# Small matmuls that rotate through strips of the array: attention blocks and a block inverse

## The chip, the core and the metric

The kernel runs on one core of a Trainium2 chip. The metric is the device time of one execution in microseconds, the median of several runs. The core has a matmul engine (PE, with PEld for its loads of the stationary operand), a vector engine (DVE), an activation engine (ACT), a general engine (POOL) and a queue that issues transfers (SP). They run side by side and wait for one another by semaphores.

## What is computed

One layer over 2048 latent tokens and 256 context tokens, width 1024: a modulated layer norm, one wide input projection, two linear-attention branches, each in both directions over the tokens, and gated output projections with a residual layer norm. The two places that matter here, cut from the reference:

```python
def gla_chunk_scan(q, k, v, g, s0):          # branch B, f_t and k_t = 1 - f_t
    ...
    qg = q * jnp.exp(G)
    kg = k * jnp.exp(-G)
    attn = jnp.where(incl, jnp.einsum('bhncd,bhnsd->bhncs', qg, kg), 0.0)
    ...
    o_c = einsum(qg_c, S) + einsum(attn_c, v_c)
    S = S * gl_c + einsum(kd_c, v_c)

def gdn_chunk_scan(q, k, v, g, beta, s0):    # branch A, the gated delta rule
    ...
    a_mat = jnp.where(strict, jnp.einsum('bhncd,bhnsd->bhncs', kb, k) * decay, 0.0)
    sol = lax.linalg.triangular_solve(a_mat + eye, rhs, left_side=True, lower=True, unit_diagonal=True)
    ...
```

Branch B needs, per head, direction and chunk, a triangular matrix `attn`. Branch A needs, per head, direction and chunk, the inverse of a unit triangular matrix.

## The kernel before

Everything is fp32. The large projections are three matmuls of a split operand each (`proj`, lines 211 to 213, moving operand 128x512). The small matmuls of this study are plain fp32, and the trace shows each of these as two passes: two records of a weight load and a matmul.

The array can be used in strips of 32. Which strips a matmul takes follows from its operands: the partitions from which it reads its operands give the row strip, the partitions of PSUM to which it writes give the column strip. A stationary operand 32 wide over 128 partitions takes one column strip of four (the profile writes 128*32); one 64 wide takes two (128*64); a 32x32 block takes one row strip and one column strip (32*32), here called a tile of the array.

**Branch B, `scan_group`** (from line 502). For each of 4 heads and 2 directions it goes over 4 groups of 512 latent tokens and one of the context. A latent group holds four chunks of 128 tokens, and each chunk's 128x128 matrix `attn` is made in `pat` (PSUM, four chunks side by side) from blocks: 16 products of 32x32 on the diagonal for the four chunks; then, per chunk `i`, two 32x32 blocks across (k = 0, 1; operands `a` and `b32`) and one 64x64 block across (operands `a64` and `b64`). The helper `mm` sets which operand is stationary: `b` in direction 0, `a` in direction 1. So a block lands on the partitions, and in the column strips, of its `b` tokens in direction 0 and of its `a` tokens in direction 1. When all are done, line 610 copies `pat` under a mask into `atB` (DVE), which line 619 uses. There are 32 latent groups in all. While they run, PE also carries the projections of the next group, of the next head (`head_units`) and of a gate (`gate_units`).

**Branch A, `levels`** (from line 809). The 128x128 inverse of each of 18 chunks is put together from the inverses of its 32x32 diagonal blocks (made by `solve` on DVE): five stages of small matmuls, each followed by a copy out of PSUM.

- L828: 16 matmuls 32x32, four tiles of the array (`pairs`), four heads each, then the copy to `yt` (DVE, L830)
- L834: 8 matmuls 32x32, two tiles, then a copy to `N64` (DVE, L837)
- L840: 16 matmuls 32x32, four tiles, then copies to `Nb` (ACT, L842)
- L847: 8 matmuls 64x64, two tiles (`hs`), then the copy to `yt2` (DVE, L849)
- L852: 8 matmuls 64x64, two tiles, then copies to `Nb` (ACT, L854)

All write to one PSUM tile `lvt` of 128 partitions by 512 floats. In each stage the loop over tiles is outside and the loop over heads inside, so four matmuls in a row use the same tile of the array. Between the stages stand `prep` of later chunks, `stepA` (the recurrence of branch A, line 931) and gate projections (`gate_block`, L211 to L213).

What sets the order: the program is written in stages as above, and a scheduler with its own estimate of times fixes the order on each engine when the kernel is built. On the chip each engine follows that order.

Of the kernel before, what the change touches and what calls it, by code (L numbers as in the profile page):

```python
# [24 lines left out]
H = 4  # L25
# [14 lines left out]
def block_kernel(ctx, tc, x, c, ctx_in, c_ctx, w_mod, b_mod, w_in, conv_w, a_log, dt_bias,  # L40
# [442 lines left out]
    with tc.tile_pool(name="rb", reuse_waits="tile", bufs=1, side="right") as rb, \  # L483
# [12 lines left out]
        def bl(a):  # L496
            return slice(32 * a, 32 * a + 32)

        def b4(t):
            return t.rearrange("p c (b t) -> p c b t", t=32)  # L500

        def scan_group(h, d, g, ps, S):
# [4 lines left out]
            s = rb.tile([P, GT], F32, tag="s", name="s", bufs=2)[:, :n]  # L507
# [51 lines left out]
            a = X.rearrange("p (c t) -> p c t", t=P)  # L559
# [9 lines left out]
            def fb(f, m):  # L569
                return f.unsqueeze(3).to_broadcast([P, k_, m, 32])  # L570
# [18 lines left out]
            if lat:  # L589
                a64 = rb.tile([P, 4, 64], F32, tag="a64", name="a64")  # L590
                b64 = rb.tile([P, 4, 64], F32, tag="b64", name="b64")
                b32 = rb.tile([P, 4, 64], F32, tag="b32", name="b32")
                ve.tensor_tensor(out=b4(a64), in0=b4(a)[:, :, 2:4], in1=fb(f2, 2), op=ALU.mult)
                po.tensor_tensor(out=b4(b64), in0=b4(b)[:, :, 0:2], in1=fb(f3, 2), op=ALU.mult)
                po.tensor_tensor(out=b4(b32), in0=b4(b)[:, :, 0:4:2], in1=fb(f4, 2), op=ALU.mult)

                def mm(i, am, bm, asl, bsl):
                    if d == 0:
                        te.matmul(out=pat[bsl, i, asl], lhsT=bm, rhs=am, start=True, stop=True)
                    else:  # L600
                        te.matmul(out=pat[asl, i, bsl], lhsT=am, rhs=bm, start=True, stop=True)

                for i in range(4):
                    for k in range(4):
                        mm(i, a[:, i, bl(k)], b[:, i, bl(k)], bl(k), bl(k))
                for i in range(4):
                    for k in range(2):
                        mm(i, a[:, i, bl(2 * k + 1)], b32[:, i, bl(k)], bl(2 * k + 1), bl(2 * k))
                    mm(i, a64[:, i, :], b64[:, i, :], slice(64, 128), slice(0, 64))
                ve.copy_predicated(out=atB[d], mask=mk[d].unsqueeze(1).to_broadcast([P, 4, P]), data=pat)  # L610
                o = rb.tile([P, 4, P], F32, tag="o", name="o")
                if d == 1:
                    sy.dma_start(out=o, in_=oP[h, g])
                pw = pb.tile([P, 4, P], F32, tag="o", name="pw")
                qg = ag if d == 0 else bg
# [54 lines left out]
        for h in range(H):  # L670
            fill = head_units(h + 1) if h + 1 < H else gate_units(NEARLY + GA)
            for d in range(2):
                w = load_w((C_FF, C_FB)[d] + h * P)
                S = None
                for j, g in enumerate(((4, 0, 1, 2, 3), (4, 3, 2, 1, 0))[d]):
                    S = scan_group(h, d, g, proj(w, g), S)
                    for _ in range(FBI[d][j] if h + 1 < H else FB[j] * d):
                        next(fill, None)
            for _ in fill:
                pass  # L680
# [18 lines left out]
    with tc.tile_pool(name="rc", reuse_waits="tile", bufs=2, side="right") as rc, \  # L699
# [109 lines left out]
        def levels(pos):  # L809
            ch = seq[pos]  # L810
            Nb, N64 = Nbs[pos % 2], N64s[pos % 2]
            an = rc.tile([P, H, 96], F32, tag="an2", name="an2", bufs=1)
            sy.dma_start(out=an, in_=anD[ch])
            tx = [rc.tile([P, 2, H, 32], F32, tag=f"n{i}", name=f"n{i}", bufs=1) for i in range(2)]
            for i in range(2):
                sy.dma_start(out=tx[i].rearrange("p d h j -> p (d h) j"), in_=nD[i][pos].rearrange("d h b i j -> (b i) (d h) j"))
            n3 = [tx[1 - d][:, d] for d in range(2)]
            nt = [tx[d][:, d] for d in range(2)]
            for b in range(4):
                for d in range(2):  # L820
                    (ve, po)[d].tensor_copy(out=Nb[bl(b), d, :, bl(b)], in_=n3[d][bl(b)])
                ac.copy(out=N64[bl(b), :, bl(b % 2)], in_=nt[b // 2][bl(b)])
            pairs = [(d, 2 * p + d, 2 * p + 1 - d) for d in range(2) for p in range(2)]
            lvt = pc.tile([P, H, 128], F32, tag="lv", bufs=1, name="lvt")
            py, pn = (lvt[:, :, 32 * i:32 * i + 32] for i in range(2))
            for d, s, t in pairs:
                for h in range(H):
                    te.matmul(out=py[bl(t), h, :], lhsT=an[bl(s), h, 0:32], rhs=nt[d][bl(s), h, :], start=True, stop=True)  # L828
            yt = rc.tile([P, H, 64], F32, tag="yt", name="yt", bufs=1)
            ve.tensor_copy(out=yt[:, :, 0:32], in_=py)  # L830
            for d, s, t in pairs:
                if s // 2 == d:
                    for h in range(H):
                        te.matmul(out=pn[bl(t), h, :], lhsT=n3[d][bl(t), h, :], rhs=yt[bl(t), h, 0:32], start=True, stop=True)  # L834
            for d, s, t in pairs:
                if s // 2 == d:
                    ve.tensor_copy(out=N64[bl(t), :, bl(s % 2)], in_=pn[bl(t)])  # L837
            for d, s, t in pairs:
                for h in range(H):
                    te.matmul(out=pn[bl(s), h, :], lhsT=yt[bl(t), h, 0:32], rhs=n3[d][bl(t), h, :], start=True, stop=True)  # L840
            for d, s, t in pairs:
                ac.copy(out=Nb[bl(s), d, :, bl(t)], in_=pn[bl(s)])  # L842
            hs = [(d, slice(64 * d, 64 * d + 64), slice(64 - 64 * d, 128 - 64 * d)) for d in range(2)]
            pn, py = lvt[:, :, 0:64], lvt[:, :, 64:128]
            for d, s, t in hs:
                for h in range(H):
                    te.matmul(out=py[t, h, :], lhsT=an[s, h, 32:96], rhs=N64[s, h, :], start=True, stop=True)  # L847
            yt = rc.tile([P, H, 64], F32, tag="yt", name="yt2", bufs=1)
            ve.tensor_copy(out=yt, in_=py)  # L849
            for d, s, t in hs:  # L850
                for h in range(H):
                    te.matmul(out=pn[s, h, :], lhsT=yt[t, h, :], rhs=Nb[t, d, h, t], start=True, stop=True)  # L852
            for d, s, t in hs:
                ac.copy(out=Nb[s, d, :, t], in_=pn[s])  # L854
            sy.dma_start(out=atN[ch, :, :, 1], in_=Nb)

        grp = [(c0, min(CG, NC - c0)) for c0 in range(0, NC, CG)]
        for i in range(len(grp) + 2):
            pl = list(range(grp[i][0], sum(grp[i]))) if i < len(grp) else []
            ll = list(range(grp[i - LAG][0], sum(grp[i - LAG]))) if 0 <= i - LAG < len(grp) else []  # L860
            if IL == 0:
                for ch in pl:
                    prep(ch)
                for ch in ll:
                    levels(ch)
            elif IL == 3:
                for ch in ll:
                    levels(ch)
                for ch in pl:
                    prep(ch)  # L870
            else:
                while pl or ll:
                    if pl:
                        prep(pl.pop(0))
                    if ll:
                        levels(ll.pop(0))
                        if IL == 2 and ll:
                            levels(ll.pop(0))
            if 0 <= i - LAG + 1 < len(grp):
                solve(*grp[i - LAG + 1])  # L880
# [20 lines left out]
    if True:  # L901
        SA = []
        for d in range(2):
            t = rd.tile([P, H, P], F32, tag=f"S{d}", name=f"S{d}")
# [291 lines left out]
```

## Time and profile before

| | |
|---|---|
| median of 3 runs | 2302.93 us (2299.16 to 2306.05) |
| the profiled execution | 2301.48 us, its span 2299.7 us |
| PE busy | 2201.6 us (96% of the span) |
| DVE, ACT, POOL busy | 1391.9, 912.9, 734.8 us |
| granted PE clock, mean | 0.985 |
| branch B stage | about 525 to 1063 us of the span |
| `levels` | 1225 to 1690 us of the span |

How to read it: a PE row's time is the union of its matmuls, and each matmul's duration holds the pipeline's depth (about 0.19 us for a 32-wide one), so many of them overlap. What a series of matmuls costs is read from the starts: from its first start to the start of the matmul that follows. In a row of the timeline that holds several records, the first column is the first start, the second the time from there to the last end.

### The profile page before, as it was taken

The page shows a single profiled execution, that of the slowest core. Times are in us where ns is not written, and L with a number is a line of the kernel's source. Part 1 is how long each engine was busy: PE and PEld are TensorE (multiplying, and loading weights), DVE is VectorE, ACT ScalarE, POOL GpSimd, SP SyncE. Part 2 cuts the span into 40 slices and gives each one's busy share as a digit, 9 for nine tenths or more (in the row PEclk, how much of TensorE's full clock was granted, in tenths as well). Part 3 has the DMA queues.
Part 4 walks back from the last instruction along what each step waited for, and adds up shares of the span by engine and source line. Part 5 has one row for each costly group of instructions (what it writes and reads, how often), then busy time and mean ns, then how long its engine had stood idle before and what let it go on. Part 6 is the DMA issues. An engine that isn't in the chain of part 4 may idle for free. (4 is left out here: it accounts for less than half of the span.)

```text
span 2299.7 us, 39916 instructions
## 1 busy us (share of the span) xinstructions
PE 2201.6 (96%) x14998; PEld 1843.8 (80%) x14998; DVE 1391.9 (61%) x3198; ACT 912.9 (40%) x2312; POOL 734.8 (32%) x736
## 2 busy tenths in 40 slices
PE   7899999999999999999999999999989988999998
PEld 2778888888888888888877787888878877888887
DVE  5926666627675776784464858774332337766565
ACT  3522222233343443442434454544444345434441
POOL 3614333312221221214544454421114223432331
PEclk8999999999999999999999999999999999999999
DMA  8312222322322322223656577877788765344432
GB/s 317 107 42 72 68 69 74 90 69 68 95 75 71 106 70 82 81 80 114 182 158 185 176 233 248 256 213 209 229 265 281 246 217 188 120 139 136 126 109 78
DMA packets 298328, 330.24 MB, mean 144 GB/s; under 512 B 77535, under 2 KB 216917, under 8 KB 298135
## 3 DMA queue, kind: packets, MB, share of 16 engines
q1 hardware_dynamic: 296119, 320.35, 45.3%
q0 software_dynamic: 2016, 7.34, 0.9%
q8 instruction: 118, 1.93, 0.4%
q14 instruction: 75, 0.61, 0.1%
HBM read 216.83 MB, written 110.79 MB: 142 GB/s over the span
## 5 line engine op out<-in xcount | busy, mean ns | idle before, releaser
L211 PE MATMUL ps<-uhi,wh 128*128 128x512 f32 (+1 forms) x1824 | 707.3, 388 | 6.4 <-DVE uhi L299 2.7
L212 PE MATMUL ps<-ulo,wh 128*128 128x512 f32 (+1 forms) x1824 | 705.4, 387 | 2.8 <-DVE ulo L301 2.6
L213 PE MATMUL ps<-uhi,wl 128*128 128x512 f32 (+1 forms) x1824 | 705.5, 387 | 0.5 <-POOL wl L203 0.5
L211 PEld LDWEIGHTS ps<-uhi,wh 128*128 128x128 f32 x1824 | 345.2, 189 | 72.0 <-DVE uhi L299 3.8
L212 PEld LDWEIGHTS ps<-ulo,wh 128*128 128x128 f32 x1824 | 345.4, 189 | 66.4 <-DVE ulo L301 3.7
L213 PEld LDWEIGHTS ps<-uhi,wl 128*128 128x128 f32 x1824 | 344.9, 189 | 64.0 <-POOL wl L203 0.9
L203 POOL TENSOR_TENSOR wl<-ws,wh 128x512 fp32r<-128x512 f32 x144 | 192.2, 1335 | 536.3 <-ACT wh L202 515.5
L202 ACT CAST wh<-ws 128x512 fp32r<-128x512 f32 x144 | 89.5, 622 | 286.1 <-DMA ws<-in_w_in_dram 193.6
L399 DVE SCALAR_TENSOR_TENSOR acc<-raw,cols,acc 128x512 f32<-128x512 f32 x192 | 153.9, 855 | 0.9
L1095 PE MATMUL py<-yh,wab 128*128 128x256 f32 x512 | 146.1, 287 | 8.5 <-DVE mg L1098 7.6
L1097 PE MATMUL py<-yh,wab 128*128 128x256 f32 x512 | 144.4, 282 | 0.0
L1096 PE MATMUL py<-yl,wab 128*128 128x256 f32 x512 | 144.3, 282 | 0.0
L578 POOL TENSOR_TENSOR bg<-s,fz 128x512 f32<-128x512 f32 (+1 forms) x36 | 37.8, 1049 | 263.4 <-ACT X L558 97.5
L1114 PE MATMUL pso<-uhi,mh 128*128 128x512 f32 x256 | 102.8, 403 | 7.2 <-ACT mh L1100 3.2
L1095 PEld LDWEIGHTS py<-yh,wab 128*128 128x128 f32 x512 | 97.5, 191 | 10.9 <-DVE mg L1098 9.2
L1116 PE MATMUL pso<-uhi,ml 128*128 128x512 f32 x256 | 101.8, 398 | 0.6 <-DVE ml L1101 0.6
L1115 PE MATMUL pso<-ulo,mh 128*128 128x512 f32 x256 | 101.5, 397 | 0.0
L1096 PEld LDWEIGHTS py<-yl,wab 128*128 128x128 f32 x512 | 97.6, 191 | 0.4
L1097 PEld LDWEIGHTS py<-yh,wab 128*128 128x128 f32 x512 | 97.6, 191 | 0.2
L1078 POOL TENSOR_TENSOR yl<-gt,yh 128x512 fp32r<-128x512 f32 x32 | 44.5, 1393 | 149.1 <-ACT yh L1077 149.1
L402 POOL TENSOR_TENSOR acc<-acc,sg 128x512 f32<-128x512 f32 (+1 forms) x56 | 71.5, 1295 | 46.3 <-ACT sg L401 46.3
L1088 ACT ACTIVATE mg<-mg 128x512 f32<-128x512 f32 x64 | 40.4, 632 | 112.0 <-DMA mg<-gT 112.0
(373 smaller groups left out, 4097.8 us busy)
## 6 DMA issues: line engine op xcount, KB each, us to landing
ws<-in_w_in_dram SPq DMA_DIRECT2D x144, 256.0 KB, 3.2
gT<-gt SPq DMA_DIRECT2D x96, 256.0 KB, 3.2
kv<-knvD SPq DMA_DIRECT2D x36, 512.0 KB, 5.2
kq<-qkvD SPq DMA_DIRECT2D x32, 512.0 KB, 5.6
an<-atN SPq DMA_DIRECT2D x32, 512.0 KB, 6.0
mg<-gT SPq DMA_DIRECT2D x64, 256.0 KB, 3.5
qkvD<-acc SPq DMA_DIRECT2D x48, 256.0 KB, 2.3
l<-qkvD SPq DMA_DIRECT2D x16, 768.0 KB, 5.1
```

What stands on the lines that cost most here:

```text
L202: ac.copy(out=wh[:, j:j + 4, :], in_=ws)
L203: po.tensor_tensor(out=wl[:, j:j + 4, :], in0=ws, in1=wh[:, j:j + 4, :].bitcast(F32), op=ALU.subtract)
L211: te.matmul(out=ps, lhsT=wh[:, k, :], rhs=uhi[gi][:, k, :], start=(k == 0), stop=False)
L212: te.matmul(out=ps, lhsT=wh[:, k, :], rhs=ulo[gi][:, k, :], start=False, stop=False)
L213: te.matmul(out=ps, lhsT=wl[:, k, :], rhs=uhi[gi][:, k, :], start=False, stop=(k == KB - 1))
L399: ve.scalar_tensor_tensor(out=a_, in0=raw[:, o + k:o + k + n], scalar=wk, in1=a_, op0=ALU.mult, op1=ALU.add)
L1095: te.matmul(out=py[:, i, :], lhsT=wh[:, k, ms_], rhs=yh[i][:, k, :], start=(k == 0), stop=False)
L1096: te.matmul(out=py[:, i, :], lhsT=wh[:, k, ms_], rhs=yl[i][:, k, :], start=False, stop=False)
L1097: te.matmul(out=py[:, i, :], lhsT=wl[:, k, ms_], rhs=yh[i][:, k, :], start=False, stop=(k == H - 1))
L1114: te.matmul(out=ps, lhsT=mh[:, k, ts_], rhs=wout[0][k][:, ns], start=(k == 0), stop=False)
L1115: te.matmul(out=ps, lhsT=mh[:, k, ts_], rhs=wout[1][k][:, ns], start=False, stop=False)
L1116: te.matmul(out=ps, lhsT=ml[:, k, ts_], rhs=wout[0][k][:, ns], start=False, stop=(k == KB - 1))
```

## The change

Two edits, both on PE alone.

1. In `scan_group`, the 64x64 block across becomes two matmuls with a stationary operand 32 wide and a moving operand 64 wide, so that all blocks use strips of 32. The order of the four matmuls of a chunk is set by direction: column strips 0, 2, 0, 1 in direction 0 and 3, 1, 3, 2 in direction 1.
2. In `levels`, all five loops have the heads outside and the tiles of the array inside.

```diff
+                def across32(i, k):
+                    mm(i, a[:, i, bl(2 * k + 1)], b32[:, i, bl(k)], bl(2 * k + 1), bl(2 * k))
+
+                def across64(i, k):
+                    if d == 0:
+                        mm(i, a64[:, i, :], b64[:, i, bl(k)], slice(64, 128), bl(k))
+                    else:
+                        mm(i, a64[:, i, bl(k)], b64[:, i, :], bl(2 + k), slice(0, 64))
...
                 for i in range(4):
-                    for k in range(2):
-                        mm(i, a[:, i, bl(2 * k + 1)], b32[:, i, bl(k)], bl(2 * k + 1), bl(2 * k))
-                    mm(i, a64[:, i, :], b64[:, i, :], slice(64, 128), slice(0, 64))
+                    across32(i, d)
+                    across32(i, 1 - d)
+                    across64(i, d)
+                    across64(i, 1 - d)
...
-            for d, s, t in pairs:
-                for h in range(H):
+            for h in range(H):
+                for d, s, t in pairs:
                     te.matmul(out=py[bl(t), h, :], lhsT=an[bl(s), h, 0:32], rhs=nt[d][bl(s), h, :], start=True, stop=True)
...
-            for d, s, t in hs:
-                for h in range(H):
+            for h in range(H):
+                for d, s, t in hs:
                     te.matmul(out=py[t, h, :], lhsT=an[s, h, 32:96], rhs=N64[s, h, :], start=True, stop=True)
```

The loops of L834, L840 and L852 change in the same way as those of L828 and L847 shown here. Eleven lines are added ahead of `levels`, so what is L828, L834, L840, L847, L852 before is L839, L845, L851, L858, L863 after.

The order on PE around a group of branch B before (`pk` is a transpose, `pw` the output; `X` and `s` hold `a` and `b`, `b_...` here is `b32` beside `X`, and `b64` beside `a_...`, which is `a64`):

```order
L583 MATMUL pk<-ident,bg 128x128 x4
L599 MATMUL pat<-X,s 32x32 x16
L599 MATMUL pat<-X,b_4169 32x32 x2
L599 MATMUL pat<-a_4167,b_4168 64x64
L599 MATMUL pat<-X,b_4169 32x32 x2
L599 MATMUL pat<-a_4167,b_4168 64x64
```

And such a group after:

```order
L583 MATMUL pk<-ident,bg 128x128 x4
L599 MATMUL pat<-X,s 32x32 x11
L599 MATMUL pat<-X,b_4484 32x32 x2
L599 MATMUL pat<-a_4482,b_4483 32x64 x2
L599 MATMUL pat<-X,b_4484 32x32 x2
L599 MATMUL pat<-a_4482,b_4483 32x64 x2
```

One block of 64x64 has become two of 32x64; what stands around the group is the same, and how many of the 16 diagonal blocks come ahead of the transposes differs from group to group in both kernels.

The order on PE at the first stage of `levels` for one chunk, before (`n` with its two numbers are the two sets of inverted blocks):

```order
L213 MATMUL ps<-uhi_414,wl 128x512
L828 MATMUL lvt<-n_10815,an_10813 32x32 x8
L828 MATMUL lvt<-n_10816,an_10813 32x32 x8
L725 MATMUL pk<-ident,l 128x128 x4
L732 MATMUL pq<-ident,l 128x128 x4
```

And after:

```order
L213 MATMUL ps<-uhi_309,wl 128x512
L839 MATMUL lvt<-n_10943,an_10941 32x32 x2
L839 MATMUL lvt<-n_10944,an_10941 32x32 x2
L839 MATMUL lvt<-n_10943,an_10941 32x32 x2
L839 MATMUL lvt<-n_10944,an_10941 32x32 x2
L839 MATMUL lvt<-n_10943,an_10941 32x32 x2
L839 MATMUL lvt<-n_10944,an_10941 32x32 x2
L839 MATMUL lvt<-n_10943,an_10941 32x32 x2
L839 MATMUL lvt<-n_10944,an_10941 32x32 x2
L736 MATMUL pk<-ident,l 128x128 x4
```

The 16 matmuls of the stage stand together as before and alternate between the sets. The number of gate projections between the last stages of two successive chunks stays within one or two (the count of L211 ahead of the ninth chunk's last stage is 1586 before and 1584 after). On the other engines, rows move by a few places near these points and no instruction is added or removed.

More of the change, by code (lines that the diff above doesn't have):

```diff
@@ L830, in levels @@
             ve.tensor_copy(out=yt[:, :, 0:32], in_=py)
-            for d, s, t in pairs:
-                if s // 2 == d:
-                    for h in range(H):
+            for h in range(H):
+                for d, s, t in pairs:
+                    if s // 2 == d:
                         te.matmul(out=pn[bl(t), h, :], lhsT=n3[d][bl(t), h, :], rhs=yt[bl(t), h, 0:32], start=True, stop=True)
@@ L837, in levels @@
                     ve.tensor_copy(out=N64[bl(t), :, bl(s % 2)], in_=pn[bl(t)])
-            for d, s, t in pairs:
-                for h in range(H):
+            for h in range(H):
+                for d, s, t in pairs:
                     te.matmul(out=pn[bl(s), h, :], lhsT=yt[bl(t), h, 0:32], rhs=n3[d][bl(t), h, :], start=True, stop=True)
@@ L844, in levels @@
             pn, py = lvt[:, :, 0:64], lvt[:, :, 64:128]
-            for d, s, t in hs:
-                for h in range(H):
+            for h in range(H):
+                for d, s, t in hs:
                     te.matmul(out=py[t, h, :], lhsT=an[s, h, 32:96], rhs=N64[s, h, :], start=True, stop=True)
@@ L849, in levels @@
             ve.tensor_copy(out=yt, in_=py)
-            for d, s, t in hs:
-                for h in range(H):
+            for h in range(H):
+                for d, s, t in hs:
                     te.matmul(out=pn[s, h, :], lhsT=yt[t, h, :], rhs=Nb[t, d, h, t], start=True, stop=True)
```

## The prediction

> **What bounds the kernel now.** I read the page's busy line first, then the busy time by stages, then who PE waits for in the two stages that the change touches, and last the timeline of PE around one group and one chunk.
>
> ```profile
> PE 2201.6 (96%) x14998; PEld 1843.8 (80%) x14998; DVE 1391.9 (61%) x3198; ACT 912.9 (40%) x2312; POOL 734.8 (32%) x736
> ...
> core 0: us, PE busy (x) PEld busy (x) DVE busy (x) ACT busy (x) POOL busy (x), PEclk, DMA share, GB/s
> 525.00:1063.00 538.00, 535.02 (x4337) 447.63 (x4337) 378.93 (x1030) 215.53 (x393) 121.90 (x125) 1.00 0.28 83
> 1225.00:1690.00 465.00, 445.57 (x4016) 373.22 (x4015) 289.14 (x821) 225.90 (x746) 158.12 (x202) 0.98 0.73 220
> ```
>
> In the branch B stage PE is idle for 3 us of 538, in the `levels` stage for 19 of 465. No other engine is near: DVE has 70% and 62%. The order on each engine is fixed, so in these stages the time is the sum of what PE's instructions take, plus those few waits. The waits themselves, from the list of who waited for whom on PE in each stage:
>
> ```profile
> PE pk L583 <- POOL bg L578: 0.9, 1, 0.9
> PE pat L599 <- ACT s L551: 0.9, 1, 0.9
> PE pS L588 <- DMA v<-vB: 0.7, 1, 0.7
> PE pw L618 <- DVE S L624: 0.4, 1, 0.4
> ...
> PE lvt L852 <- DVE yt L849: 9.4, 6, 2.7
> PE pq L732 <- DVE an L769: 1.7, 1, 1.7
> ```
>
> Four waits in the first stage, each under 1 us: a PE that gets faster there turns that into time. In the second, 6 of the 18 chunks already find `yt` late at L852.
>
> **Part 1, the blocks of branch B.** Timeline of PE over one group in direction 0, and the durations of its matmuls (least, median, most in ns) from the view of the tile `pat`:
>
> ```profile
> 537.17 0.46 PE L599 MATMUL pat<-X,s 128*32 128x32 f32 x32
> 537.45 0.26 PE L599 MATMUL pat<-X,b 128*32 128x32 f32 x4
> 537.63 0.33 PE L599 MATMUL pat<-a,b 128*64 128x64 f32 x2
> 537.89 0.26 PE L599 MATMUL pat<-X,b 128*32 128x32 f32 x4
> 538.08 0.33 PE L599 MATMUL pat<-a,b 128*64 128x64 f32 x2
> 538.33 0.26 PE L599 MATMUL pat<-X,b 128*32 128x32 f32 x4
> 538.52 0.33 PE L599 MATMUL pat<-a,b 128*64 128x64 f32 x2
> 538.78 0.26 PE L599 MATMUL pat<-X,b 128*32 128x32 f32 x4
> 538.96 0.33 PE L599 MATMUL pat<-a,b 128*64 128x64 f32 x2
> 539.22 0.38 PE L618 MATMUL pw<-S,ag 128*128 128x128 f32 x1
> ...
> L599 PE MATMUL pat<-X,s x512: 196/196/218, 524.7 to 1000.0; 128*32 128x32 f32 x171
> ```
>
> The 32 passes of the diagonal, which go round four strips, take 0.46 us to the last end, so 0.46 - 0.196 = 0.26 us from first to last start: 8 passes in each strip, about 32 ns each, four strips side by side. The 24 passes of the blocks across take from 537.45 to 539.22, 1.77 us, in four equal rounds of 0.44 us (537.89, 538.33, 538.78). In a round the four 32-wide passes need 0.26 - 0.20 = 0.06 us between starts; the rest, 0.38 us, goes into two 64-wide passes and the change of shape before and behind them.
>
> After, all 64 passes of a group use strips of 32. Per round there are eight passes, and one strip has four of them (0 in direction 0, 3 in direction 1): two with a moving operand of 32 and two of 64. The first kind takes 32 ns in a strip, as above. The second is not in the trace. Its bounds: as the first (32 ns) or the whole 64-wide pass with its drain, half of 0.38 us. A moving operand of 64 against 32 costs 26 ns by the durations of two 128-row matmuls:
>
> ```profile
> L599 PE MATMUL pat<-a,b x128: 222/246/271, 526.3 to 1003.1; 128*64 128x64 f32 x128
> ```
>
> 222 less 196 is 26, so I take 32 + 26 = 58 ns. A round is then 2 x 32 + 2 x 58 = 180 ns for the busiest strip, with the other strips beside it, four rounds 0.72 us, and some 0.10 us to leave the shape at the end (now 539.22 less the last 64-wide start). 1.77 - 0.82 = 0.95 us per group, 30.4 us over 32 groups; some groups are cut by other matmuls and pay an entry more, in both kernels, so 30 us.
>
> What hides behind this? `atB` is copied by DVE when the last block is done, and an output matmul (L619) waits for it. That copy waits for the blocks and is late for nobody: in the list of the stage no matmul waits for it. With 30 us gone from 538, DVE stands at 379 of 508, 75%, and next to be late would be `bg` (L578) or `s` (L551), the two that PE waited for 0.9 us. I take no loss here, 3 us at most.
>
> **Part 2, the five loops of `levels`.** Four of the stages of one chunk in the timeline, and the durations of their passes from the view of the tile `lvt`:
>
> ```profile
> 1294.45 0.89 PE L828 MATMUL lvt<-n,an 32*32 32x32 f32 x32
> 1299.49 0.59 PE L834 MATMUL lvt<-yt,n 32*32 32x32 f32 x16
> 1305.26 0.89 PE L840 MATMUL lvt<-n,yt 32*32 32x32 f32 x32
> 1310.15 0.96 PE L847 MATMUL lvt<-N,an 64*64 64x64 f32 x16
> ...
> L828 PE MATMUL lvt<-n,an x576: 184/191/258, 1225.0 to 1680.7; 32*32 32x32 f32 x192
> L847 PE MATMUL lvt<-N,an x288: 218/218/308, 1246.0 to 1686.3; 64*64 64x64 f32 x144
> ```
>
> From first to last start: L828 and L840 0.89 - 0.19 = 0.70 us, L834 0.40, L847 0.96 - 0.22 = 0.74. After, L828 and L840 are four tiles with eight passes each, one head of all four tiles at a time: the pattern of the 32 diagonal passes, 0.26 us. Saved: 0.44 each. L834 is two tiles with eight passes each, which is the same series with two strips left out: 0.25, saved 0.15. L847 and L852 are two tiles with eight 64-wide passes each, 8 x 58 = 0.46, saved 0.28 each. Sum 0.44 x 2 + 0.15 + 0.28 x 2 = 1.59 us a chunk, 28.6 us over 18 chunks.
>
> The cover is thinner than in part 1. Behind each stage stands a copy on DVE or ACT that the next stage needs, but gate projections stand between the stages (L828 at 1294.45, L834 at 1299.49: 5 us), so an earlier end seldom changes when the next starts. Where L852 already waits for `yt` (6 of 18 chunks), PE comes earlier and waits longer; the price is between 0 and 6 x 1.59 = 9.5 us, and I take the middle, 5 us. The transfers have 0.73 of their engines in this stage, and would have 0.73 x 465 / 441 = 0.77.
>
> A rule speaks against this part. All tiles of a stage write to one PSUM tile, `lvt`, on different partitions, and their operands lie in different row strips. In the trace two such tiles do run together: L847 has 16 passes of 58 ns, 0.93 us if one followed the other, and takes 0.74; L834 has 16 of 32 ns, 0.51, and takes 0.40; where the loop goes from one tile to the next, their passes overlap. The Trainium skill (TensorEngine Tiling (Array Packing), Gotcha 1: PSUM Pressure) says that different row tiles cannot access the same PSUM bank simultaneously; by that rule the tiles of a stage would take turns and rotating would gain nothing. The trace disagrees for two tiles, and shows nothing of four.
>
> **The sum.** 30 + 28.6 - 5 = 53.6 us off the profiled 2301.48 us is 2248; the median of the runs lies 1.5 us above the profiled one, so 2249, which I round to 2250 us.
>
> **Rivals.**
>
> *Row strips take turns at the one PSUM tile.* Then every pass of `levels` follows the one before it: 32 x 32 = 1.02 us for L828 and L840 (0.32 more than now), 0.51 for L834 (0.11 more), 0.93 for L847 and L852 (0.19 more): 1.13 us x 18 = 20 us lost against the 30 of part 1, 2293. For it: four at once stand nowhere in the trace. Against: the 0.74 and 0.40 above. In a milder form two run together and four do not: L828 and L840 then take 0.51, 0.19 saved each, the rest as forecast, 1.09 x 18 = 20 us, and 2302.9 - 30 - 20 + 5 = 2258, which lies inside the main range.
>
> *The waits eat part 2.* DVE does `solve` in the same stage and `yt` stands in its queue behind it. If PE's gain in `levels` all turns into waiting at L852 and L834, part 1 alone is left: 2302.9 - 30 = 2273. For it the 9.4 us above, against it that 12 chunks of 18 do not wait at all and that PE has only 19 us idle in 465.
>
> *A strip pays its reload in full.* Two strips with two passes each need 0.06 us between starts (the 0.26 rows), so the first reload in a strip costs about 55 ns instead of 32. If a strip that other strips interrupt always pays that, a round of part 1 is 2 x 55 + 2 x 81 = 272 ns and part 1 gains 0.95 - 4 x 0.09 = 0.59 us, 19 us; L828 and L840 take 8 x 55 = 0.44 (saving 0.26), L834 0.44 too (0.04 more), L847 and L852 8 x 0.107 = 0.86 (0.12 more each; 0.107 is the step between two 64-wide passes, 0.33 - 0.222 in the row of 537.63): 0.24 x 18 = 4 us. 2302.9 - 23 = 2280. Against it: the 32 diagonal passes go round four strips and keep 32 ns.
>
> *Slower.* The same reload, and no strip running beside another while weights change: every pass costs its 55 ns (107 for a 64-wide one) alone. A round of part 1 is 4 x 55 + 4 x 81 = 544 ns against 440 now, 13 us more in all; `levels` takes 80 x 55 + 32 x 107 = 7.8 us a chunk against 0.70 x 2 + 0.40 + 0.74 x 2 = 3.3, 81 us more: 2397. It decides from where the mean step of L828 passes that of now, 0.70 / 31 = 23 ns. The diagonal passes have 0.26 / 31 = 8 ns, which all but excludes it.
>
> *The order.* The scheduler could have moved other work so that PE waits. The order on PE shows the same gate projections between the chunks within two; a chance remains, at no change.
>
> **Chances.** Both parts as forecast, with two or four tiles at once and waits from 0 to 9.5 us: 0.68, 2240 to 2262. Waits eat part 2, 2262 to 2276: 0.15. Turns at PSUM, to 2293: 0.05. Reload in full, about 2280: 0.05. No change: 0.03. Slower: 0.04. The low end takes the full 58.6 us and 4 us of shorter waits elsewhere (2240), and a little below; the high end reaches past the second case: 2238 to 2278. Within 0.3% of before, 7 us, counts as no change, about what a measurement of this kernel can tell. Faster 0.93, same 0.03, slower 0.04.
>
> **What the profile after would show.** Part 1: the rows of one group of `pat` from the first block across to the next matmul in 0.8 us, and in the busy time of `pat` in its stage about 30 us less than the 77 of now; 0.6 us less per group means the reload. Part 2: 32 passes of the first stage of `levels` in 0.46 us to the last end (0.70 with two tiles at once, over 1.2 with turns), the 64-wide stages in 0.68. If the passes are as short as that and the stage is still as long, the waits at the fourth and fifth stage will have grown from 9.4 us.
>
> ```profile
> 525.00:1063.00 538.00, 77.18 (x1777) 55.97 (x1776) 22.87 (x31) 1.00 0.28 83
> ```
>
> That row is the busy time of PE, PEld and DVE on `pat` alone. What would make the forecast wrong: a PE that cannot be fed 64 passes in a microsecond (the longest close series now is 32), or a DVE that is late in the first stage.

## The result and the profile after

The changed kernel takes 2264.35 us (2262.43 to 2270.93, 4 runs), the one before 2302.94 us: 38.6 us less, a ratio of 0.9838 with the interval 0.9813 to 0.9863. The forecast was 2250 us in a range of 2238 to 2278. The time lies inside the range, 2 us above what was given to the likeliest case (2240 to 2262) and at the low edge of the case in which waits eat part 2 (2262 to 2276). It is 14 us above the 2250 of the sum.

The profiled execution took 2265.5 us, its span is 2263.6. The page's busy line, and the busy time by stage in the columns of before; the last two rows cut the `levels` stage near the start of the eleventh chunk:

```profile
PE 2155.3 (95%) x15254; PEld 1806.4 (80%) x15254; DVE 1386.2 (61%) x3198; ACT 912.6 (40%) x2312; POOL 737.0 (33%) x736
```

```profile
core 0: us, PE busy (x) PEld busy (x) DVE busy (x) ACT busy (x) POOL busy (x), PEclk, DMA share, GB/s
525.00:1033.00 508.00, 503.11 (x4554) 426.37 (x4556) 376.16 (x1027) 215.25 (x392) 122.85 (x124) 1.00 0.30 87
...
1193.00:1502.00 309.00, 286.18 (x2448) 234.76 (x2447) 211.55 (x597) 157.28 (x529) 133.47 (x164) 0.96 0.74 220
1502.00:1656.00 154.00, 143.54 (x1585) 120.14 (x1584) 75.16 (x225) 70.03 (x225) 26.22 (x42) 0.96 0.76 229
```

The branch B stage is 30 us shorter, 508 for 538, and PE has 5 us of idle in it for 3 before. The `levels` stage is 463 us for 465, with 33 us of idle PE for 19 and a granted clock of 0.96 for 0.98. So the first part of the change came out as time, and most of the second did not.

That is not because the second part's matmuls failed to get shorter. One group of `pat` in direction 0, from its first block across (558.39) to the matmul behind the group (559.19), and the stages of one chunk of `levels`:

```profile
558.23 0.36 PE L599 MATMUL pat<-X,s 128*32 128x32 f32 x19
558.39 0.20 PE L599 MATMUL pat<-X,b 128*32 128x32 f32 x1
...
558.44 0.22 PE L599 MATMUL pat<-a,b 128*32 128x64 f32 x1
...
558.98 0.28 PE L599 MATMUL pat<-a,b 128*32 128x64 f32 x3
559.19 0.38 PE L629 MATMUL pw<-S,ag 128*128 128x128 f32 x1
```

```profile
1298.81 0.45 PE L839 MATMUL lvt<-n,an 32*32 32x32 f32 x32
...
1304.19 0.44 PE L845 MATMUL lvt<-yt,n 32*32 32x32 f32 x16
...
1307.93 0.45 PE L851 MATMUL lvt<-n,yt 32*32 32x32 f32 x32
...
1313.73 0.68 PE L858 MATMUL lvt<-N,an 64*64 64x64 f32 x16
```

The blocks across take 0.80 us (1.77 before), the first and third stage of `levels` 0.45 us to the last end (0.89), the second 0.44 (0.59), the fourth 0.68 (0.96). All of these are the forecast's numbers to 0.02 us. Busy time on `pat` in its stage, and the first and last start of the first stage of `levels` (its columns: least, median and most of the duration in ns, then those starts):

```profile
525.00:1033.00 508.00, 46.35 (x1999) 35.66 (x2002) 22.78 (x31) 1.00 0.30 87
```

```profile
L839 PE MATMUL lvt<-n,an x576: 184/191/212, 1193.5 to 1648.4; 32*32 32x32 f32 x192
```

On `pat` 30.8 us went (77.18 to 46.35). The first stage of `levels` starts 31.5 us earlier in the first chunk (1225.0 to 1193.5) and 32.3 us earlier in the last (1680.7 to 1648.4): from the first chunk to the last the second part brought 1 us there.

What PE waited for in the `levels` stage, in us, times and the longest:

```profile
PE lvt L863 <- DVE yt L860: 9.8, 6, 3.8
PE lvt L851 <- DVE N L848: 3.5, 2, 3.1
PE psA L942 <- DVE r L954: 3.4, 3, 1.4
PE lvt L839 <- DMA an<-anD: 2.4, 1, 2.4
PE psA L942 <- DVE S L961: 2.4, 2, 2.0
PE pq L743 <- DVE an L780: 1.9, 2, 1.6
```

The wait for `yt` that the forecast spoke of stands where it stood (9.4 before, the fifth stage). The new idle time is spread over many small waits.

To separate the causes I added up, over the records of PE in the stage (first matmul of the first chunk to the last of the last chunk), the time from each start to the next, with the part in which PE had drained (no matmul was running) and the part at half the granted clock. The column of the half clock leaves drained time out; the loss is half of all the time at half clock.

| | stage | PE drained | at half clock | lost to the clock |
|---|---|---|---|---|
| before | 463.6 us | 18.8 | 16.3 | 8.8 |
| after | 461.7 us | 32.3 | 35.8 | 18.8 |

The matmuls on `lvt` take 26.5 us less (72.1 to 45.6). Of that, 13.5 us became drained time and some 10 us went to the clock; 2 us are left. (The rows of the profile give 19.4 and 33.3 us without a matmul, 13.9 between them, which agrees.)

### The profile page after: what moved, and what is told of

The parts are those of the page before. It is cut to its first block, busy times and chain, and to the rows that moved or that the text cites. A ratio compares the mean times of both kernels' runs of the same rounds, so it can differ in the third digit from the quotient of the medians.

```text
span 2263.6 us, 40408 instructions
## 1 busy us (share of the span) xinstructions
PE 2155.3 (95%) x15254; PEld 1806.4 (80%) x15254; DVE 1386.2 (61%) x3198; ACT 912.6 (40%) x2312; POOL 737.0 (33%) x736
## 5 line engine op out<-in xcount | busy, mean ns | idle before, releaser
L211 PE MATMUL ps<-uhi,wh 128*128 128x512 f32 (+1 forms) x1824 | 707.7, 388 | 4.1 <-DVE uhi L299 2.8
L211 PEld LDWEIGHTS ps<-uhi,wh 128*128 128x128 f32 x1824 | 346.1, 190 | 69.9 <-DVE uhi L299 3.8
```

The lines of the kernel that those rows point to most:

```text
L211: te.matmul(out=ps, lhsT=wh[:, k, :], rhs=uhi[gi][:, k, :], start=(k == 0), stop=False)
```

## The experiments

Beside the times I use one table, worked out from the records: by how many us each kernel is ahead of the profiled execution before at six places. Those are the first `prep` of a chunk, the first matmul of `levels` in chunks 1, 11, 15 and 18, and the last matmul of `stepA`.

| kernel | median us | prep | chunk 1 | chunk 11 | chunk 15 | chunk 18 | last `stepA` |
|---|---|---|---|---|---|---|---|
| after | 2264.35 | 29.4 | 31.5 | 34.0 | 34.5 | 31.9 | 33.0 |
| part 1 alone (e1) | 2284.78 | 28.5 | 29.2 | 30.9 | 23.7 | 15.5 | 15.7 |
| part 2 alone (e2) | 2287.12 | 1.4 | 2.5 | 5.6 | 8.3 | 5.4 | 9.1 |
| part 1, short `solve` (e3) | 2256.20 | 27.2 | 67.6 | 70.0 | 63.9 | 40.0 | 38.7 |
| both, short `solve` (e4) | 2235.04 | 29.7 | 69.9 | 80.4 | 81.9 | 63.0 | 66.4 |
| later pieces (e5) | 2274.16 | 29.3 | 31.5 | 36.3 | 36.7 | 7.2 | 28.1 |
| `yt` on ACT (e6) | 2266.32 | 28.5 | 30.1 | 42.3 | 45.8 | 34.6 | 34.8 |
| same strip (e7) | 2266.71, one run | 28.4 | 29.1 | 35.9 | 35.6 | 33.4 | 32.9 |
| regrouped (e8) | 2279.20, one run | 25.6 | 27.9 | 27.6 | 28.3 | 25.7 | 22.6 |
| ACT, PB 14 (e9) | 2266.11 | 28.7 | 29.2 | 40.5 | 43.7 | 9.8 | 37.6 |
| ACT, PB 12 (e10) | 2259.20 | 28.9 | 30.4 | 44.1 | 47.4 | 30.7 | 39.6 |
| after again (e11) | 2264.63 | 28.0 | 29.0 | 34.3 | 34.9 | 33.6 | 36.3 |
| ACT, PB 12 again (e12) | 2258.67 | 27.8 | 28.8 | 43.2 | 47.3 | 31.7 | 45.2 |

**The parts one at a time.** Part 1 alone, with the five loops of `levels` as before:

```diff
-            for h in range(H):
-                for d, s, t in pairs:
+            for d, s, t in pairs:
+                for h in range(H):
```

(and so in the other four). 

> The blocks of branch B alone are changed; the five loops of levels stand as before. Theory A (a PE that is faster in the levels stage only waits more, so all of the gain is the blocks'): 2266 to 2272 us, 31 to 37 under before. Rival B (each part gives about half of the 38 us): 2280 to 2286.

Measured: 2284.78 us (2283.97 to 2285.66) against 2298.28 for the kernel before on the same chip, ratio 0.9947 (0.9932 to 0.9961), 13.5 us. Theory A's number fell and rival B's held. The trace says where it went. Up to the eleventh chunk the kernel is 30.9 us ahead. The loss lies in the last chunks, and most of it is the clock. The `levels` stage in two windows, of this kernel and of the one before, cut near the start of the eleventh chunk (0.4 us ahead of it in the first, 3 us in the second):

```profile
1196.00:1507.00 311.00, 297.35 (x2444) 247.09 (x2441) 215.94 (x596) 156.89 (x528) 132.68 (x163) 0.98 0.73 219
1507.00:1674.00 167.00, 159.19 (x1580) 135.98 (x1579) 75.62 (x226) 70.42 (x224) 26.54 (x42) 0.92 0.70 210
```

```profile
1225.00:1535.00 310.00, 295.75 (x2438) 245.62 (x2437) 215.11 (x600) 156.11 (x523) 132.94 (x161) 0.98 0.73 219
1535.00:1690.00 155.00, 149.83 (x1581) 127.60 (x1579) 74.03 (x222) 69.79 (x223) 25.18 (x41) 0.99 0.73 222
```

167 us at a granted clock of 0.92 are 154 us at full clock, 155 us at 0.99 are 153. Taken by the records from the eleventh chunk's first matmul to the last of `levels`, this kernel needs 166.5 us and the one before 151.6, 15 us more: 11 are the half clock (13.1 lost against 1.8), and 4 are 17 matmuls of projections more that stand there (266 against 249, at 0.235 us). Part 1 gained its 28.5 us, and stretches at half clock (the longest lasts 17 us, from 1637) took some 11 of them.

Part 2 alone, with the blocks of branch B as before:

```diff
-                    across32(i, d)
-                    across32(i, 1 - d)
-                    across64(i, d)
-                    across64(i, 1 - d)
+                    for k in range(2):
+                        mm(i, a[:, i, bl(2 * k + 1)], b32[:, i, bl(k)], bl(2 * k + 1), bl(2 * k))
+                    mm(i, a64[:, i, :], b64[:, i, :], slice(64, 128), slice(0, 64))
```

> The five loops of levels alone are changed. Theory A: the 28 us that PE no longer needs there turn into waits for DVE and into time at half clock; 2296 to 2303 us, at most 7 under before. Rival B: 2280 to 2286.

Measured: 2287.12 us (2285.44 to 2289.28), ratio 0.9957 (0.9942 to 0.9973), 11.2 us: theory A's number fell, and rival B's was missed by 1 us, though waits and half clock, as A had them, are what the trace shows. The matmuls on `lvt` take 26 us less here too (46.5). PE is drained for 33.0 us of the stage (18.8 before) and at half clock for 33.7 (16.3). Its waits:

```profile
PE lvt L852 <- DVE yt L849: 15.0, 7, 4.1
PE pk L725 <- DMA l<-qkvD: 4.4, 2, 3.6
PE pq L732 <- DVE an L769: 2.9, 2, 2.5
```

So the drained time belongs to part 2: it is 20.7 with part 1 alone, 33.0 with part 2 alone, 32.3 with both. The half clock does not belong to it alone: 37.7 us with part 1 alone. The parts by themselves bring 13.5 and 11.2 us, 24.7 in all and 14 less than the 38.6 of both; they did not run beside the changed kernel, but as shares of the kernel before that ran beside each it is the same (0.5 and 0.4% against 1.6%).

**Is it `solve`?** Both kernels again, with 4 of the 31 steps of `solve` on DVE:

```diff
-            for j in range(31):
+            for j in range(0, 31, 8):
```

> The blocks as after, levels as before, and solve cut to 4 of its 31 steps (its output is left wrong): takes some 24 of 28 us of DVE out of each of 5 series. Theory A1 (solve on DVE paces the levels stage): the stage gets shorter by 30 us or more, since PE is not its bound, or PE becomes the bound at its 445 us busy. Theory A2 (the loop of prep over its single buffers paces it): the stage shortens by less than 10 us.

> Both parts as after, and solve cut to 4 of its 31 steps (its output is left wrong). A1: without solve PE is the bound, and this run is 18 to 28 us under the run with the same cut and the loops of levels as before. A2: it is within 8 us of that run.

Measured: 2256.20 us (2252.66 to 2259.39) and 2235.04 us (2234.32 to 2237.6), ratios 0.9817 (0.9798 to 0.9836) and 0.9732 (0.9717 to 0.9746). The cut is worth 28.6 us with part 1 and some 25 with both (63.2 against 38.6, each under the kernel before that ran beside it), and on top of it part 2 is worth 21.2 us, near the 23.6 of the forecast (28.6 less 5). The times fit A1 of the second text. The `levels` stage itself did not get shorter: from its first matmul to its last it takes 491 us with part 1 and the cut, 478 with part 1 alone, since it starts 38 us earlier and takes in 121 matmuls of projections more (28 us). So the stage's length decides nothing between A1 and A2 of the first text.

The 21.2 us read as if `solve` had eaten part 2. The traces do not bear it out for the greater part. From the first matmul of chunk 1 to that of chunk 11 the two kernels have the same number of projections on PE, and the stretch is 310.8 us in the one and 302.8 in the other; PE is drained for 6.5 us in the one and for 14.8 in the other. The kernels with the whole `solve` have 313.3 and 310.8 us there (before and after), drained 13.9 and 22.3. The growth by part 2 is the same, 8.3 and 8.4 us. Over the whole stage it is 9 us with the short `solve` (12.6 to 21.7) and 12 to 14 with the whole, so about a third of the new waits at most can be put down to `solve`. What differs more is the time at half clock: 8.0 to 6.2 us in that stretch with the short `solve`, 13.9 to 22.5 with the whole. And with the whole `solve` part 2 on top of part 1 brings as much, 20 us by the medians and 25 against the kernels before, of which some 11 are what the half clock had taken from part 1 alone. `solve` on DVE costs time (the cut brings 25 to 29 us), but it is not what turns most of part 2's gain into waits.

**The wait that the profile names.** The copies to `yt` go to ACT, which is busy for 40% and does not carry `solve`:

```diff
-            ve.tensor_copy(out=yt[:, :, 0:32], in_=py)
+            ac.copy(out=yt[:, :, 0:32], in_=py)
...
-            ve.tensor_copy(out=yt, in_=py)
+            ac.copy(out=yt, in_=py)
```

> Both parts as after; the copies to yt (the first and the fourth of levels) are made by ACT instead of DVE, so they no longer stand behind the series of solve in DVE's queue. Theory A1 (PE's waits behind solve on DVE took the gain of levels): the 11.5 us that PE waits for yt go, 2251 to 2259. Rival: ACT is as late, or the waits move to the other copies on DVE: 2260 to 2268.

Measured: 2266.32 us (2262.58 to 2267.64) against 2304.08, ratio 0.9834 (0.9818 to 0.9851): no different from the changed kernel. Its first waits on PE in `levels`, and that for `yt`:

```profile
PE lvt L858 <- ACT Nb L853: 5.0, 2, 3.4
PE pv L754 <- DVE dec L787: 3.2, 5, 1.6
...
PE lvt L863 <- ACT yt L860: 2.8, 2, 1.5
```

The two waits for `yt`, 11.5 us together in the changed kernel (9.8 and 1.7), are down to 2.8. PE's drained time in the stage is 32.6 us, as before the edit (32.3): the sum is what it was, over other waits. The lead of 42 to 46 us in chunks 11 and 15 looks like a gain and is none. The scheduler put 230 instead of 245 triples of gate projections between chunks 1 and 11, and 16 instead of 2 between chunks 15 and 18. Fifteen triples are 11 us (46 matmuls whose starts lie 0.235 us apart), as much as the whole difference.

**The end of `levels`.** Between chunks 15 and 18 there are next to no gate projections. `PB` says after how many late gate projections the last weights begin to be prepared:

```diff
-    PB = 11
+    PB = 14
```

> Both parts as after; the weight pieces of the last stage, which pass through the same staging buffer as the gate weights, start after 14 gate blocks instead of 11, so that more gate projections are left for the end of levels, where PE has none and its clock halves. Theory C (the end of levels loses time to a PE that is too sparsely fed, at half clock): the half-clock stretch of 10 us near 1637 us goes, 2254 to 2260. Rival D (the chain of levels and the recurrence bounds that end, and projections moved there are missing later): 2261 to 2268.

Measured: 2274.16 us (2264.42 to 2275.68), ratio 0.9859 (0.983 to 0.9888), above the ranges of both theories; the remedy failed. Now 50 triples of projections stand between chunks 15 and 18 instead of 2. They delay the last chunks (lead 36.7 at chunk 15, 7.2 at chunk 18) by 29 us, and the half clock at the end of the stage is gone, but of the 48 triples taken from behind it only part comes back (28.1 at the last `stepA`, 33.0 in the changed kernel).

Both edits together, with PB 14 and with PB 12:

> The changed kernel with both copies to yt on ACT and the last weight pieces three gate projections later (PB 14 for 11), the two edits that were tried alone before. Theory F: what took the gain of the copies back was that no gate projections were left for PE between the last four chunks of levels; with projections left there the lead of the middle (46 to 50 us over before) is kept, and the time is 2250 to 2258. Rival G: the last chunks wait for the recurrence and for the solve of their own chunk, and projections put there only delay levels, as they did with the later pieces alone: 2268 to 2276, with a lead at chunks 15 to 17 of under 25 us.

> The same with one gate projection later (PB 12). Theory F: a part of it, 2257 to 2262. Rival G: 2264 to 2270, no better than the changed kernel (2264) and the same as with the copies alone (2266).

Measured: 2266.11 us (2262.31 to 2266.33), ratio 0.9833 (0.9815 to 0.985), and 2259.20 us (2256.75 to 2260.65), ratio 0.9803 (0.9784 to 0.9822). With PB 14 the lead goes from 43.7 at chunk 15 over 32.2 and 19.3 to 9.8 at chunk 18, so it is under G's 25 from chunk 17 only; the time is 2 us under G's range, and F's 2250 to 2258 fell. With PB 12 the time is in F's range, but not for F's reason: the lead of the middle is not kept (47.4 at chunk 15, 30.7 at chunk 18). With PB 12 there are 32 triples between chunks 15 and 18, 16 more than with the copies alone, at a price of 11 us; the lead at chunk 18 falls by 4 us only (34.6 to 30.7), so some 7 us of them lie where PE would have been idle or slow (between chunks 15 and 18 drained time and clock loss account for 5 of these: drained 4.8 to 2.4 us, lost 3.4 to 1.1). Behind the stage, 16 fewer triples bring back 9 us (from 30.7 to 39.6, where the copies alone stay at 35). The net is 5 us.

The changed kernel and this version had run on different chips; both ran once more, on one:

> The changed kernel itself, on one chip beside the version with the yt copies on ACT and PB 12, since the two stand on different chips so far (ratios to before 0.9838 and 0.9803, whose intervals overlap). Theory: 0.983 to 0.985 of before here too. Rival, that the 5 us between them are the chip's: the same ratio as the other, within 0.002.

> The yt copies on ACT and PB 12, a second time. Theory: 0.980 to 0.981 of before, 5 us (3 to 8) under the changed kernel of the same call. Rival: the same as the changed kernel within 0.002.

Measured: 2264.63 us (2262.16 to 2268.17), ratio 0.9845 (0.983 to 0.986), and 2258.67 us (2254.49 to 2265.49), ratio 0.9819 (0.9799 to 0.9839). The distance of 6 us came back, and the difference of the ratios, 0.0026, is above the rival's 0.002; the ratio 0.9819 itself is above the 0.980 to 0.981 expected, and the intervals still overlap a little. The version with the copies on ACT and PB 12 has the lowest median with all of the work in it, by 5 to 6 us in both comparisons; that it is the faster one is likely and not certain. The page's span of it and its last `stepA`, beside that of the changed kernel (the profiled execution of this version is its shortest, 2254.49 us, so these rows show more than the 6 us):

```profile
span 2252.6 us, 40411 instructions
```

```profile
L942 PE MATMUL psA<-vv,an x256: 270/275/377, 1457.5 to 1815.9; 128*128 128x128 f32 x128
```

```profile
L942 PE MATMUL psA<-vv,an x256: 270/275/422, 1449.5 to 1828.1; 128*128 128x128 f32 x128
```

**What made the blocks of branch B shorter?** Two kernels ask whether it was the rotation. In the first, the order within a round puts two matmuls of the same strip in a row (0, 0, 1, 2 in direction 0):

```diff
                     across32(i, d)
-                    across32(i, 1 - d)
                     across64(i, d)
                     across64(i, 1 - d)
+                    across32(i, 1 - d)
```

> Both parts as after, but the four blocks of a chunk run in strips 0, 0, 1, 2 (direction 1: 3, 3, 2, 1), so that two in a row share a strip. Theory E (the busiest strip's passes set the time and the order does not matter): the blocks across of a group take 0.75 to 0.90 us as after. Rival F (two in a row in one strip stall those behind them): 1.0 us or more.

In the second, the kernel before keeps its 64x64 blocks and only does the eight 32x32 blocks of a group first and the four of 64x64 behind them:

```diff
                 for i in range(4):
                     for k in range(2):
                         mm(i, a[:, i, bl(2 * k + 1)], b32[:, i, bl(k)], bl(2 * k + 1), bl(2 * k))
+                for i in range(4):
                     mm(i, a64[:, i, :], b64[:, i, :], slice(64, 128), slice(0, 64))
```

> The kernel before, with the 64x64 blocks kept, but all eight 32-wide blocks of a group ahead of all four 64-wide ones: one change of shape instead of seven. If the changes of shape are the larger part of the 0.95 us per group: the blocks across take 1.0 to 1.1 us instead of 1.77 (0.26 + 0.13 + 0.107 + 7 x 0.058 + 0.15). If each 64-wide pass takes its 0.107 us anyway: 1.4 us.

Measured in one run each: 2266.71 us, the same as the changed kernel, and 2279.20 us against 2304.08 before. Busy time on `pat` in the stage, first of the one, then of the other, and the timeline of a group of the second (a group that other work cuts in two):

```profile
525.00:1033.00 508.00, 46.46 (x2008) 35.65 (x2008) 22.75 (x31) 1.00 0.29 87
```

```profile
525.00:1040.00 515.00, 52.43 (x1760) 41.20 (x1760) 23.43 (x32) 1.00 0.29 87
```

```profile
545.08 0.32 PE L599 MATMUL pat<-X,b 128*32 128x32 f32 x8
545.33 0.45 PE L599 MATMUL pat<-a,b 128*64 128x64 f32 x4
545.70 0.49 PE L619 MATMUL pw<-S,ag 128*128 128x128 f32 x2
```

46.46 us for 46.35: this order within the round costs nothing, and theory E's number held (0.80 to 0.82 us for the blocks across of a group that other work does not cut, by the records; 0.80 to 0.85 in the changed kernel). 52.43 us: of the 30.8 us that went from `pat`, 24.8 go by the regrouping alone. Blocks across that are not cut take 0.97 to 1.01 us there, at the low end of the 1.0 to 1.1 expected, so of the 0.97 us a group by which the change shortens them (1.77 to 0.80), 0.80 come with changing between 32-wide and 64-wide strips once a group instead of seven times, and 0.17 with 32-wide strips in place of the 64-wide blocks. The lead of this kernel is 25.6 us at the first `prep` and 25.7 us at chunk 18: with 23 us at half clock in the stage (18 before, 40 with part 1 alone; drained time counted in), what the regrouping saves passes through `levels` nearly whole. That is a second witness, in one run, that part 1 alone was set back by the clock.

## Why the prediction was right, and where it was off

**Part 1: right in size and in conversion.** 30 us were forecast; `pat` gave 30.8, and the lead at the first `prep` is 29.4. The model behind it, the busiest strip with 32 and 58 ns a pass, gave 0.82 us a group against 0.80, and e7 shows that the order within the round does not matter. That the busiest strip sets the pace fits the records (the rounds follow each other every 0.175 us in the group shown, 0.180 by the model), but no run varied that strip's work. The cover argument (no matmul of the stage waits for the copy, DVE at 75%) held: 5 us of PE idle for 3, DVE at 376 of 508. It held to the end of the kernel only beside part 2: alone, part 1 kept 13.5 us. What the prediction did not say is that most of the saving is the change of shape: it put 0.38 us of a round down to "two 64-wide passes and the change of shape" without parting them. e8 parts them.

**Part 2: the passes right, the time not.** 28.6 us of shorter passes were forecast, 26.5 came. The weighing of the rule against the trace came out on the trace's side: four tiles that write to one PSUM tile do run together (0.45 us for 32 passes; by turns it would have been 1.02 and more). The rivals of turns at PSUM, in both forms, of the reload in full and of the slower kernel fell with the same rows.

**The step that failed is the price of the waits.** "The price is between 0 and 6 x 1.59 = 9.5 us, and I take the middle, 5 us" stands against 13.5 us measured (drained time 18.8 to 32.3). Two things were wrong in it. It counted only the chunks that already waited at the fifth stage, on the ground that "gate projections stand between the stages (...), so an earlier end seldom changes when the next starts". That sentence argues against the gain as much as for it: where something else sets when the next stage starts, a shorter stage before it is idle time. And it looked for the wait at one place, `yt`, which stayed at 9.8 us; the sign given for this case, that the waits at the fourth and fifth stage would have grown from 9.4, did not show in that form either. The growth is spread over the other rows of the list, and taking the largest of them away (e6) left the sum where it was.

**A term was missing.** The granted clock was carried over from before, and it fell from 0.98 to 0.96 in the stage, 10 us. Without that the kernel would have stood at about 2254, inside the likeliest case. In the second profile of the same kernel (e11) the loss to the clock in the stage is 15.4 us instead of 18.8, so a part of it is chance.

The records say more: this term hangs on the waits. The granted clock changes on a grid of 3.41 us. In the `levels` stages of the 14 profiles the half clock sets in 72 times, and in each of the 72 windows of 3.41 us just ahead PE had drained for 0.7 to 3.4 us (median 2.0). Counted the other way, of 1589 such windows at full clock with under 0.6 us drained none was followed by half clock, of 53 with 1.5 to 2.0 us 32 were, and of 34 with 2.0 us or more all were. So 10 us of clock and 13.5 us of waits are one price, that of waits that stand close together, and the forecast had 5 us for it. This is what went together in the records; no run set such a wait alone.

**Luck.** That the time lies inside the range is partly luck. The range reached to 2278 for a case with another sign, all of part 2 lost to waiting at the second and fifth stage, and these waits hardly grew (1.4 to 1.7 and 9.4 to 9.8 us).

The sum, put right: 29.4 at the first `prep`, 26.5 from the passes of `levels`, less 13.5 of waits, less 10 of clock, is 32.4. The lead at the end of `levels` is 34.2 and at the end of the kernel 36.1, in the profiled executions. Part 2 alone, 11.2 us, and the 25.6 to 28.5 us that part 1 and the regrouping have at the first `prep`, not the 13.5 that part 1 keeps alone, add up to the 38.6 of the medians, give or take 2.

**What stays open.** What paces PE in `levels` when `yt` is early and `solve` is short is not settled. The transfers of `an` and `l` are a candidate (`an` 2.4 us after, `l` 4.4 us in e2); second buffers for them were not tried. Part 1 alone has little drained time (20.7 us) and the most at half clock (37.7). Its seven stretches too begin behind 0.8 to 3.0 us drained in a window; what is long in it is the stretch of 17 us from 1637, where PE has no projections between the small matmuls. In all 14 profiles the 44 windows at half clock that hold five or more matmuls of projections were each the last of their stretch, and of the 62 with fewer, 34 were followed by another. Where 96 or more matmuls of projections stand between chunks 15 and 18 (six profiles, e5 among them) there are at most 3.4 us at half clock there, with 48 or fewer 7 to 17 us, but none in the kernel before. Why the scheduler's small moves leave such waits close together in one kernel and not in another stays open.

## What to carry to other kernels

A saving came out at its length in a stage where PE idles for 3 us in 538, and for the lesser part (2 us of 26.5 in the stage of the changed kernel, 11 us of the whole time with part 2 alone) where PE already idles for 19 us in 465 at many small waits: there the pace is partly set elsewhere, and the wait that tops the list is not the one to remove, since others stand right behind it. Before splitting small matmuls into narrower ones, order them by shape: one change between widths a group instead of seven gave four fifths of what the split and the rotation gave together. And when an edit seems to gain in the middle of a stage, count the filler work between the same two places first: the 11 us that e6 gained on the changed kernel up to chunk 15 were 15 triples of projections put off.

## What the runs showed of the hardware

- A change between 32-wide and 64-wide strips costs: the blocks across of a group take 1.77 us with seven of them and 0.97 us with one, the same matmuls, so some 0.13 us each (an estimate, 0.80 us over six changes).
- Passes in different strips start 0.26 us apart in all for 32 of them (8 ns each), also when all four strips write to one PSUM tile on different partitions. Two matmuls in a row in the same strip cost nothing extra in the mix of e7.
- The clock was granted at half speed in stretches of 3.4 us or a few of them, and the half clock set in only behind a window of 3.4 us in which PE had drained for 0.7 us or more, always behind one with 2.0 us (34 of 34), in 32 of 53 behind one with 1.5 to 2.0, and never behind one with under 0.6 (none of 1589), in the `levels` stages of 14 profiles. No single wait has to last that long: ahead of 11 of the 72 times no wait in the window was as long as 1.0 us, and the waits in it came to 0.7 to 1.9 us together.
- In the changed kernel the half clock costs 48.7 us of full-speed time in the whole span (35.4 before), without an edit to the work that runs in most of it, and 42.4 us in its second profile. A difference of 10 us between two kernels of this length can be the clock alone, as for the greater part with part 1 alone.
